# Who makes the high part: every third piece of turned probabilities read from PSUM once, and split on GpSimd

## The chip, the cores and the metric

The kernel runs on one core of one Trainium2 chip. The core has five engines, each with an instruction queue of its own that runs in order: TensorE (PE; its weight loads are shown apart as PEld), VectorE (DVE), ScalarE (ACT), GpSimd (POOL) and SyncE (SP), which issues all loads and stores here. The metric is device time in microseconds (us) of one execution; of the kernel before there are three timed runs, and one profiled execution. The programs are put in order at build time by a scheduler that fills each engine's queue; what an engine does next is fixed from then on, and semaphores make it wait where data or a buffer is missing.

## The reference

One layer of a streaming encoder with 2048 positions of width 1024, in float32. Two attention branches run beside each other and are merged:

```python
xn = rms_norm(h, norm_gain[layer])
proj = xn @ w_in[layer]                       # q, k, v, gates, indexer
ya = chunked_relpos_attention(qa, ka, va, rel_bias) * silu(ga)   # own chunk of 64 and 8 before it
yb = dsa_sparse_attention(qb, kb, vb, iq, ik, iw) * silu(gb)     # 256 keys chosen for each query
merged = sigmoid(za + b0) * (ya @ w_branch_a) + sigmoid(zb + b1) * (yb @ w_branch_b)
out = rms_norm(h + merged @ w_out[layer])
```

Both branches have 8 heads of 64. In each, for a head, scores are made, turned into probabilities by a softmax, and multiplied with the values. That last product, of probabilities and values, is where the change lies.

## The kernel before, in words

TensorE multiplies in fp32r, a float32 form that keeps fewer bits. To get float32 results, an operand is kept as two tiles, a high part (the value rounded to fp32r) and a low part (the value less its high part), and the products of the parts are added up in PSUM.

The program has three stages. Up to about 1055 us it normalizes, projects (L216) and chooses the keys of branch B. From about 1070 to 1890 us it runs attention; from there on it makes the output product (L1420). The attention stage is a list of units: `a_unit` is a group of 512 queries and one head of branch A, `b_unit` is 128 queries and two heads of branch B. Each unit has loads, a part `one` and a part `two`, and the recorded program runs `one` of the next unit beside `two` of this one.

Part `one` makes scores on TensorE (L905 for A, L1014 for B), which VectorE takes from PSUM with bias or mask into the tile P while it finds the row's extreme mx (L831); then ScalarE takes the exponential in place (L909, L1017). Only two PSUM tiles hold scores.

Part `two` needs the probabilities with keys along the partitions. TensorE turns P by transposes into a PSUM tile pt (L939, L1031; up to four blocks of 128 columns, one piece; three such tiles in rotation). The function `split` then makes the piece's high part pth and low part ptl in SBUF, and TensorE multiplies both with the values into the PSUM tile O (L949 for A, L1039 for B), high part first, piece after piece. pth and ptl have three buffers each (HB = 3).

`split` is called 432 times. In two of three calls ScalarE copies pt to pth (L854) and VectorE subtracts, reading pt again (L855). In every third call (EVERY = 3, 144 of them, called turned pieces below), GpSimd does the subtraction. GpSimd does not read PSUM in this program, so ScalarE reads pt twice: once to round it into pth (L847), once to copy it as it is into an SBUF tile pf (L848, one buffer, PFB = 1); GpSimd then subtracts (L852).

What else stands in GpSimd's queue in this stage: the low part of the branch weights (dw, L1077), sums with the other branch (dt, L1090), the row sums spread out (rb, rbb; L975, L1053), and the gate product and low part of the attention output (L980, L984, L1060, L1065). `branch` (L1071) is the product of the gated attention output with w_branch_a or w_branch_b, in chunks of 128 rows; it is given out between the units.

Of the kernel before, what the change touches and what calls it, by code (L numbers as in the profile page):

```python
# [8 lines left out]
F32 = mybir.dt.float32  # L9
# [6 lines left out]
AF = mybir.ActivationFunctionType  # L16
OP = mybir.AluOpType
# [13 lines left out]
FAR = 1e30  # L31
LGC = 1.0
YB = {"a": 1, "b": 1}
EVERY, MODE = 3, 1
PFB = 1
EARLY = 400
KVO = 6
# [10 lines left out]
SPL, LEAD = 96, 8  # L48
# [33 lines left out]
def f32(ap):  # L82
    return ap.bitcast(F32)
# [11 lines left out]
def block_kernel(ctx: ExitStack, tc: tile.TileContext, io, dbg=None):  # L95
    nc = tc.nc
# [333 lines left out]
    for p, pr in enumerate(pairs):  # L430
        for k, b in enumerate(pr):
            n = 128 * (b + 1)
# [400 lines left out]
    turn = [PH]  # L833

    def split(hi, lo, src, n):
        turn[0] += 1
        if MODE == 3:
            c = n * SPL // 128
            nc.scalar.activation(hi, src, AF.Copy)
            pf = wk.tile([128, 512], F32, name="pf", tag="pf", bufs=PFB)[:, :n - c]  # L840
            nc.scalar.activation(pf, src[:, c:], AF.Copy)
            nc.vector.tensor_tensor(lo[:, :c], src[:, :c], f32(hi[:, :c]), op=OP.subtract)
            nc.gpsimd.tensor_tensor(lo[:, c:], pf, f32(hi[:, c:]), op=OP.subtract)
        elif EVERY and turn[0] % EVERY == 0:
            pf = wk.tile([128, 512], F32, name="pf", tag="pf", bufs=PFB)[:, :n]
            if MODE == 1:
                nc.scalar.activation(hi, src, AF.Copy)  # L847
                nc.scalar.activation(pf, src, AF.Copy)  # L848
            else:
                nc.scalar.activation(pf, src, AF.Copy)  # L850
                nc.gpsimd.tensor_copy(hi, pf)
            nc.gpsimd.tensor_tensor(lo, pf, f32(hi), op=OP.subtract)  # L852
        else:
            nc.scalar.activation(hi, src, AF.Copy)  # L854
            nc.vector.tensor_tensor(lo, src, f32(hi), op=OP.subtract)  # L855
# [16 lines left out]
    def a_unit(G, h):  # L872
# [39 lines left out]
        def two():  # L912
# [20 lines left out]
            for p_ in packs:  # L933
                pt = next_pt([128, 512])
                off = 0
                for kt, j0, nj in p_:
                    for j in range(j0, j0 + nj):
                        f = max(0, 4 * G + j - 4)
                        nc.tensor.transpose(pt[:, off:off + 128], P[:, j, (kt - f) * 128:(kt - f + 1) * 128], ident)  # L939
                        off += 128  # L940
                ph_ = wk.tile([128, 512], F32R, name="pth", tag="pth", bufs=HB)
                pl_ = wk.tile([128, 512], F32R, name="ptl", tag="ptl", bufs=HB)
                split(ph_[:, :off], pl_[:, :off], pt[:, :off], off)
                yield
                off = 0
                for kt, j0, nj in p_:
                    w = nj * 128
                    for n_, src in enumerate((ph_, pl_)):
                        nc.tensor.matmul(O[:, j0 * 128:j0 * 128 + w], v[:, kt - base, :], src[:, off:off + w],  # L949
                                         start=(done == 0 and n_ == 0), stop=(done == total - 1 and n_ == 1),  # L950
                                         skip_group_check=True)
                    done += 1
                    off += w
# [32 lines left out]
    def b_unit(b, u):  # L986
# [33 lines left out]
        def two():  # L1020
# [5 lines left out]
            for kt in range(0, b + 1, 2):  # L1026
                nk = min(2, b + 1 - kt)
                pt = next_pt([128, 2, 2, 128])
                for k in range(nk):
                    for e in range(2):  # L1030
                        nc.tensor.transpose(pt[:, k, e, :], P[:, e, (kt + k) * 128:(kt + k + 1) * 128], ident)  # L1031
                ph_ = wk.tile([128, 2, 256], F32R, name="pth", tag="pth", bufs=HB)
                pl_ = wk.tile([128, 2, 256], F32R, name="ptl", tag="ptl", bufs=HB)
                split(ph_.rearrange("p k n -> p (k n)")[:, :nk * 256], pl_.rearrange("p k n -> p (k n)")[:, :nk * 256],
                      pt.rearrange("p k e n -> p (k e n)")[:, :nk * 256], nk * 256)
                yield
                for k in range(nk):
                    for n_, src in enumerate((ph_, pl_)):
                        nc.tensor.matmul(o_, vBt[:, kt + k, :], src[:, k, :], start=(kt + k == 0 and n_ == 0),  # L1039
                                         stop=(kt + k == b and n_ == 1), skip_group_check=True)  # L1040
# [484 lines left out]
```

## Time and profile before

| | |
|---|---|
| timed runs (3) | 2093.07 us median, 2090.68 to 2093.47 |
| profiled execution, own time | 2089.03 us |
| its span | 2087.2 us |
| mean granted TensorE clock | 0.987 of full speed |
| busy over the span | PE 1997.9 us (96%), PEld 1693.9 (81%), DVE 1475.8 (71%), ACT 1285.5 (62%), POOL 809.9 (39%) |

The span is the time from the first to the last instruction that the profiler shows; the execution's own time is 1.8 us longer. Durations below are of this profiled execution. Busy times count an instruction from its start to its end. TensorE's matmuls overlap in its pipeline and their ends are modelled, so its busy share can be near 100% where it could still do more. In the rows of the trace, `out<-in` are the program's tile names, x is a count, and what stands in brackets is the idle time of the engine ahead of the instruction and what ended it.

### The profile page before, as it was taken

The numbers are of one execution on the slowest core, as the hardware profiler recorded it, in microseconds if no ns is written. First come the engines' busy times: TensorE is split into PE (matmuls) and PEld (weight loads), VectorE is DVE, ScalarE is ACT, GpSimd is POOL, SyncE is SP. The second block draws the span as 40 slices with busy tenths as digits, with TensorE's granted clock in tenths as the row PEclk, the third lists the DMA queues.
The fourth block names the chain that finished last, engine by engine and source line by source line (L and its number), as shares of the span: only waits on it lengthen the run. The fifth ranks groups of instructions, "written<-read, shape, count | busy, mean of one in ns | idle before, by whom it ended". The sixth has DMA issues, their size and how long they took to land.

```text
span 2087.2 us, 33654 instructions
## 1 busy us (share of the span) xinstructions
PE 1997.9 (96%) x10706; PEld 1693.9 (81%) x10706; DVE 1475.8 (71%) x3746; ACT 1285.5 (62%) x2644; POOL 809.9 (39%) x981
## 2 busy tenths in 40 slices
PE   8798999999998999999978999999999999999998
PEld 7576888889888887888867888888888888888886
DVE  6739899989798836555546678766886688865434
ACT  5465666656565544654458779866886688873221
POOL 2146322122221345545435455445444644343410
PEclk9899999999999999999989999999999999999999
DMA  9487433354545453333485664555245631145642
GB/s 359 145 290 242 166 131 123 106 176 147 178 170 175 150 184 112 116 129 119 134 237 171 203 192 143 155 177 191 88 124 178 195 109 51 58 140 191 216 134 91
DMA packets 225928, 333.77 MB, mean 160 GB/s; under 512 B 28625, under 2 KB 99665, under 8 KB 225617
## 3 DMA queue, kind: packets, MB, share of 16 engines
q1 hardware_dynamic: 225744, 331.57, 49.2%
q8 instruction: 85, 1.39, 0.3%
q14 instruction: 99, 0.80, 0.1%
HBM read 219.33 MB, written 112.16 MB: 159 GB/s over the span
## 4 chain that ended last, share of the span: by engine, by line
PE 53%; DMA 4%; DVE 2%; ACT 2%; issue 1%; POOL 1%; SPq 1%; DVEq 0%; ACTq 0%; POOLq 0%
PE acc L216 12%; PE po L1420 9%; PE d L216 8%; PE O L1039 6%; PE s L1014 5%; PE pt L1031 5%; PE O L949 3%; PE s L905 3%; PE pt L939 3%; DMA dst<-wA 1%; DMA kk<-kA 1%; DMA dst<-wB 1%; DVE P L831 1%; DMA ost<-wO 1%; DVE ptl L855 0%
## 5 line engine op out<-in xcount | busy, mean ns | idle before, releaser
L216 PE MATMUL acc<-xh,wt 128*128 128x512 f32 x1856 | 599.3, 394 | 5.7 <-DVE e L336 2.4
L216 PEld LDWEIGHTS acc<-xh,wt 128*128 128x128 f32 x1856 | 347.2, 188 | 84.4 <-DVE e L336 2.6
L216 PE MATMUL acc<-xl,wt 128*128 128x512 f32 x928 | 363.8, 393 | 0.0
L208 POOL TENSOR_TENSOR wt<-wst,wt 128x512 fp32r<-128x512 f32 (+1 forms) x108 | 145.4, 1375 | 419.8 <-ACT wt L207 303.4
L852 POOL TENSOR_TENSOR ptl<-pf,pth 128x512 fp32r<-128x512 f32 (+1 forms) x144 | 179.6, 1247 | 178.0 <-ACT pf L848 128.4
L855 DVE TENSOR_TENSOR ptl<-pt,pth 128x512 fp32r<-128x512 f32 (+1 forms) x288 | 187.3, 660 | 45.0 <-ACT pth L854 42.5
L216 PEld LDWEIGHTS acc<-xl,wt 128*128 128x128 f32 x928 | 174.5, 188 | 38.7
L485 DVE SCALAR_TENSOR_TENSOR sc<-lg,iw,sc 128x512 f32<-128x512 f32 (+2 forms) x266 | 178.6, 678 | 26.1 <-ACT lg L480 21.9
L1014 PE MATMUL s<-kBt,qsB 128*128 128x512 f32 (+3 forms) x640 | 188.0, 385 | 1.3 <-DVE mx L831 0.9
L480 ACT ACTIVATE lg<-lg 128x512 f32<-128x512 f32 (+2 forms) x304 | 147.9, 521 | 44.5 <-PE lg L478 43.6
L854 ACT ACTIVATE pth<-pt 128x512 fp32r<-128x512 f32 (+1 forms) x288 | 159.3, 578 | 25.2 <-PE pt L939 11.5
L1017 ACT ACTIVATE P<-P,mx 128x128 f32<-128x128 f32 (+15 forms) x128 | 154.3, 1207 | 20.6 <-DVE mx L831 20.1
L1031 PE MATMUL pt<-ident,P 128*128 128x128 f32 x1088 | 164.4, 273 | 1.2 <-DVE ptl L855 0.6
L1039 PE MATMUL O<-pth,vBt 128*128 128x256 f32 x544 | 146.3, 288 | 3.2 <-ACT pth L854 1.4
L1039 PE MATMUL O<-ptl,vBt 128*128 128x256 f32 x544 | 145.8, 295 | 1.8 <-POOL ptl L852 1.2
L831 DVE CUSTOM_DVE_ANT_0 P<-s,mk,mx 128x512 f32<-128x512 f32 (+2 forms) x192 | 125.0, 651 | 29.8 <-PE s L1014 24.7
L1031 PEld LDWEIGHTS pt<-ident,P 128*128 128x128 f32 x1088 | 127.0, 140 | 10.5 <-DVE ptl L855 1.1
L1077 POOL TENSOR_TENSOR dw<-dst,dw 128x512 fp32r<-128x512 f32 x64 | 82.7, 1292 | 124.5 <-ACT dw L1076 122.7
L478 PE MATMUL lg<-ikT,iqT 128*128 128x512 f32 (+2 forms) x304 | 111.3, 378 | 18.0 <-DVE sc L485 17.9
L905 PE MATMUL s<-kk,qz 128*128 128x256 f32 (+2 forms) x464 | 113.8, 341 | 15.4 <-DMA kk<-kA 7.8
L533 ACT ACTIVATE jk<-sc,st 128x640 int8<-128x640 f32 (+6 forms) x49 | 71.2, 1453 | 84.3 <-DVE st L551 73.6
L1014 PEld LDWEIGHTS s<-kBt,qsB 128*128 128x128 f32 x640 | 102.9, 190 | 15.8 <-DVE mx L831 9.1
(286 smaller groups left out, 4738.9 us busy)
## 6 DMA issues: line engine op xcount, KB each, us to landing
wst<-wP SPq DMA_DIRECT2D x100, 256.0 KB
wst<-wS SPq DMA_DIRECT2D x56, 256.0 KB
kk<-kA SPq DMA_DIRECT2D x56, 256.0 KB
vs<-vA SPq DMA_DIRECT2D x56, 256.0 KB
qz<-qA SPq DMA_DIRECT2D x96, 128.0 KB
xrow<-x SPq DMA_DIRECT2D x16, 512.0 KB
vA<-eh SPq DMA_DIRECT2D x32, 256.0 KB
dst<-wA SPq DMA_DIRECT2D x32, 256.0 KB
```

The costliest lines, as they stand in the source:

```text
L216: nc.tensor.matmul(acc, a, b, start=(first and i == 0), stop=(last and i == n - 1), **({} if first and last else {"skip_group_check": True}))
L480: nc.scalar.activation(lg, lg, AF.Relu)
L485: nc.vector.scalar_tensor_tensor(o_, lg, wv, o_, op0=OP.mult, op1=OP.add)
L852: nc.gpsimd.tensor_tensor(lo, pf, f32(hi), op=OP.subtract)
L854: nc.scalar.activation(hi, src, AF.Copy)
L855: nc.vector.tensor_tensor(lo, src, f32(hi), op=OP.subtract)
L905: nc.tensor.matmul(s_ps[:, :w], q[:, m, j * 128:(j + 1) * 128], kk[:, ko:ko + w], start=(m == 0), stop=(m == 1))
L1014: nc.tensor.matmul(s_ps[:, :w], q[:, h, :], kBt[:, m, a:a + w], start=(m == 0), stop=(m == 1))
L1017: nc.scalar.activation(P[:, e, :n], P[:, e, :n], AF.Exp, bias=mx[:, e:e + 1], scale=-1.0, accum_out=st["sum"][:, (u % 2) * 2 + e:(u % 2) * ...
L1031: nc.tensor.transpose(pt[:, k, e, :], P[:, e, (kt + k) * 128:(kt + k + 1) * 128], ident)
L1039: nc.tensor.matmul(o_, vBt[:, kt + k, :], src[:, k, :], start=(kt + k == 0 and n_ == 0), stop=(kt + k == b and n_ == 1), skip_group_check= ...
L1420: nc.tensor.matmul(accs[t, hf], a, b[:, n_], start=(k == 0 and i == 0), stop=(k == KT - 1 and i == 2))
```

## The change

For a turned piece, ScalarE now reads pt once, as a plain copy into pf. GpSimd makes the high part from pf by a copy that rounds to fp32r (a CAST in the built program), and then the low part as before. The calls of `split` that aren't turned do what they did; branches that the settings never reach are deleted as well, so that all lines behind `split` have numbers smaller by 11 (L1039 becomes L1028, L1031 becomes L1020, L1014 becomes L1003, L852 becomes L841).

```diff
-EVERY, MODE = 3, 1
+EVERY, MODE = 3, 2
...
     def split(hi, lo, src, n):
         turn[0] += 1
...
-        elif EVERY and turn[0] % EVERY == 0:
+        if turn[0] % EVERY == 0:
             pf = wk.tile([128, 512], F32, name="pf", tag="pf", bufs=PFB)[:, :n]
-            if MODE == 1:
-                nc.scalar.activation(hi, src, AF.Copy)
-                nc.scalar.activation(pf, src, AF.Copy)
-            else:
-                nc.scalar.activation(pf, src, AF.Copy)
-                nc.gpsimd.tensor_copy(hi, pf)
+            nc.scalar.activation(pf, src, AF.Copy)
+            nc.gpsimd.tensor_copy(hi, pf)
             nc.gpsimd.tensor_tensor(lo, pf, f32(hi), op=OP.subtract)
         else:
             nc.scalar.activation(hi, src, AF.Copy)
             nc.vector.tensor_tensor(lo, src, f32(hi), op=OP.subtract)
```

Beside the 144 reads less on ScalarE and the 144 casts more on GpSimd, the scheduler puts the queues of all engines in another order from the first attention unit on; nothing moves before it.

TensorE's queue early in the stage, before the change, from the transposes of one turned piece of branch B (pt_13239, 256 columns) to the product with its high part (pth_13242):

```order
L1031 MATMUL pt_13239<-ident_103,P_13164 128x128 x2
L1039 MATMUL O_13170<-ptl_13175,vBt_12324 128x256
L1031 MATMUL pt_13325<-ident_103,P_13232 128x128 x4
L1014 MATMUL s_13347<-kBt_12323,qsB_13160 128x256 x2
L1014 MATMUL s_13361<-kBt_12323,qsB_13160 128x256 x2
L1039 MATMUL O_13170<-pth_13242,vBt_12324 128x256
```

The same place after the change:

```order
L1020 MATMUL pt_13239<-ident_103,P_13164 128x128 x2
L1028 MATMUL O_13170<-ptl_13175,vBt_12324 128x256
L1020 MATMUL pt_13325<-ident_103,P_13232 128x128 x4
L1003 MATMUL s_13394<-kBt_12323,qsB_13160 128x256 x2
L1020 MATMUL pt_13351<-ident_103,P_13318 128x128 x4
L1003 MATMUL s_13411<-kBt_12323,qsB_13160 128x256 x2
L216 MATMUL d_13035<-ya0_12543,dw_13030 128x512
L1045 MATMUL pt_13379<-ident_103,rbb_13377 128x128 x2
L1003 MATMUL s_13423<-kBt_12323,qsB_13386 128x384 x2
L1003 MATMUL s_13437<-kBt_12323,qsB_13386 128x384 x2
L1028 MATMUL O_13170<-pth_13242,vBt_12324 128x256
```

Between the transposes and the product with the high part stood four rows, and now stand nine: other scores (s), the transposes of a later piece and a matmul of `branch` (d) have moved ahead of the product.

GpSimd's queue around the same piece, before:

```order
L980 TENSOR_TENSOR y_12932<-y_12932,sg_12714 128x512
L852 TENSOR_TENSOR ptl_13243<-pf_13244,pth_13242 128x256
L1060 TENSOR_TENSOR yb_13097<-yb_13097,sgB_12869 128x256
L984 TENSOR_TENSOR ya1_12544<-y_12932,ya0_12543 128x512
L1053 COPY rbb_13377<-sumB_13234 128x256
```

And after:

```order
L1042 COPY rbb_13377<-sumB_13234 128x256
L840 CAST pth_13242<-pf_13244 128x256
L973 TENSOR_TENSOR ya1_12544<-y_12932,ya0_12543 128x512
L1049 TENSOR_TENSOR yb_13097<-yb_13097,sgB_12869 128x256
L841 TENSOR_TENSOR ptl_13243<-pf_13244,pth_13242 128x256
```

The cast stands ahead of the subtraction, not always right ahead of it: here two gate operations of finished units lie between the two.

More of the change, by code (lines that the diff above doesn't have):

```diff
@@ L836, in split @@
         turn[0] += 1
-        if MODE == 3:
-            c = n * SPL // 128
-            nc.scalar.activation(hi, src, AF.Copy)
[L840 to L843, printed above, removed]
-        elif EVERY and turn[0] % EVERY == 0:
-            pf = wk.tile([128, 512], F32, name="pf", tag="pf", bufs=PFB)[:, :n]
-            if MODE == 1:
-                nc.scalar.activation(hi, src, AF.Copy)
-                nc.scalar.activation(pf, src, AF.Copy)
-            else:
-                nc.scalar.activation(pf, src, AF.Copy)
-                nc.gpsimd.tensor_copy(hi, pf)
+        if turn[0] % EVERY == 0:
+            pf = wk.tile([128, 512], F32, name="pf", tag="pf", bufs=PFB)[:, :n]
+            nc.scalar.activation(pf, src, AF.Copy)
+            nc.gpsimd.tensor_copy(hi, pf)
             nc.gpsimd.tensor_tensor(lo, pf, f32(hi), op=OP.subtract)
```

## The prediction

> **What bounds the kernel now.** I read the page's chain first, then a table of stretches over the stage that the change touches, then what TensorE waits for in it.
>
> The chain that ended last, by engine and by line:
>
> ```profile
> PE 53%; DMA 4%; DVE 2%; ACT 2%; issue 1%; POOL 1%; SPq 1%; DVEq 0%; ACTq 0%; POOLq 0%
> PE acc L216 12%; PE po L1420 9%; PE d L216 8%; PE O L1039 6%; PE s L1014 5%; PE pt L1031 5%; PE O L949 3%; PE s L905 3%; PE pt L939 3%; DMA dst<-wA 1%; DMA kk<-kA 1%; DMA dst<-wB 1%; DVE P L831 1%; DMA ost<-wO 1%; DVE ptl L855 0%
> ```
>
> TensorE's own work is the chain. ScalarE, from which the change takes a read, holds 2% of it, and GpSimd, which receives a step, 1%. The attention stage, in which all pieces are split, in stretches (columns: length, then busy time of PE, PEld, DVE, ACT, POOL):
>
> ```profile
> core 0: us, PE busy (x) PEld busy (x) DVE busy (x) ACT busy (x) POOL busy (x), PEclk, DMA share, GB/s
> 1070.00:1150.00 80.00, 67.17 (x392) 58.77 (x392) 51.18 (x181) 62.16 (x177) 41.69 (x48) 0.88 0.62 174
> 1150.00:1250.00 100.00, 96.47 (x600) 84.33 (x599) 68.07 (x198) 74.50 (x168) 53.70 (x54) 1.00 0.67 202
> 1250.00:1350.00 100.00, 98.69 (x674) 87.36 (x673) 82.83 (x236) 91.88 (x191) 53.49 (x54) 1.00 0.47 140
> 1350.00:1450.00 100.00, 97.32 (x602) 86.28 (x601) 61.67 (x163) 64.77 (x125) 52.93 (x48) 1.00 0.63 195
> 1450.00:1550.00 100.00, 97.06 (x673) 86.17 (x672) 83.95 (x235) 88.82 (x172) 41.99 (x44) 1.00 0.34 106
> 1550.00:1650.00 100.00, 99.96 (x630) 88.35 (x629) 65.82 (x172) 69.77 (x130) 49.00 (x44) 1.00 0.56 173
> 1650.00:1750.00 100.00, 98.61 (x675) 88.10 (x674) 79.60 (x222) 83.72 (x155) 47.69 (x44) 1.00 0.36 111
> 1750.00:1800.00 50.00, 49.27 (x336) 43.78 (x335) 42.76 (x117) 43.60 (x75) 20.32 (x20) 1.00 0.12 39
> 1800.00:1890.00 90.00, 86.73 (x554) 76.35 (x553) 59.52 (x123) 65.02 (x112) 36.38 (x33) 1.00 0.40 124
> sum 820.00, PE 791.28 PEld 699.49 DVE 595.39 ACT 644.24 POOL 397.18; mean PE 87.92 PEld 77.72 DVE 66.15 ACT 71.58 POOL 44.13
> ```
>
> TensorE stands idle for 820 - 791.28 = 28.7 us, 12.8 of them in the first stretch, and 740 - 724.11 = 15.9 us in all the others together. Since a busy TensorE is not one at its peak, I check this against the weight loads: at the rate of the tightest stretch (88.35 of 100 busy) the loads after 1150 (640.72 us) would fill 725 us, 15 less than the 740 they take. Both ways, about 15 us after 1150 are to be had. ScalarE reaches 92% in one stretch, but TensorE is idle there for 1.3 us only.
>
> What TensorE waited for from 1060 to 1890 (total us, times, longest; from its weight loads, then from its matmuls from 1000 on):
>
> ```profile
> PEld s L905 <- DVE mx L831: 12.1, 18, 5.5
> PEld s L1014 <- DVE mx L831: 9.1, 26, 0.7
> PEld d L216 <- ACT dw L1076: 7.6, 7, 3.1
> PEld O L1039 <- DVE ptl L855: 5.1, 17, 0.5
> PEld O L1039 <- ACT pth L854: 3.9, 6, 1.6
> PEld O L949 <- DVE ptl L855: 3.6, 10, 0.8
> PEld O L1039 <- POOL ptl L852: 1.6, 2, 1.2
> ```
>
> ```profile
> PE s L905 <- DMA kk<-kA: 7.8, 3, 4.8
> ```
>
> Few of these waits are for a turned piece (POOL ptl, 1.6 us). Most are for VectorE, which in turn waited for ScalarE's high part, in its own row:
>
> ```profile
> DVE ptl L855 <- ACT pth L854: 42.5, 44, 4.1
> ```
>
> So ScalarE reaches TensorE in two steps at most, and thinly.
>
> **The change, part by part.** One turned piece of 512 columns, as it runs now:
>
> ```profile
> 1120.81 0.59 ACT L847 ACTIVATE pth<-pt 128x512 fp32r<-128x512 f32 x1
> 1121.29 0.60 ACT L848 ACTIVATE pf<-pt 128x512 f32<-128x512 f32 x1
> 1121.97 1.29 POOL L852 TENSOR_TENSOR ptl<-pf,pth 128x512 fp32r<-128x512 f32 x1 [0.62 <-ACT pf L848]
> ```
>
> *Removed: one PSUM read.* The second read begins 0.48 us after the first, so a piece frees 0.48 us of ScalarE, not 0.60; for 256 columns it is 0.28, from the rows of the second example below. The groups give the counts:
>
> ```profile
> L848 ACT ACTIVATE pf<-pt 128x512 f32<-128x512 f32 x132 | 78.8, 597 | 0.0
> L848 ACT ACTIVATE pf<-pt 128x256 f32<-128x256 f32 x12 | 4.6, 383 | 0.0
> ```
>
> 132 x 0.48 + 12 x 0.28 = 66.7 us. ScalarE's busy time in the stage falls from 644.2 to 577.5, its idle time rises from 175.8 to 242.5. The PSUM buffer of the piece comes free 0.48 us sooner.
>
> *Added: a cast on GpSimd.* The trace of before has no cast of that size. Its nearest rows:
>
> ```profile
> L852 POOL TENSOR_TENSOR ptl<-pf,pth 128x512 fp32r<-128x512 f32 x132 | 170.7, 1294 | 173.5 <-ACT pf L848 124.8 <-PE s L1014 19.8 <-issue 7.0
> L975 POOL COPY rb<-sum 128x512 f32<-128x512 f32 x16 | 9.8, 613 | 22.9 <-DVE sum L973 21.1 <-PE pt L939 1.6
> L1053 POOL COPY rbb<-sumB 128x256 f32<-128x256 f32 x32 | 12.8, 399 | 34.6 <-DVE sumB L1051 17.1 <-PE s L1014 8.1 <-DVE mx L831 2.7
> L852 POOL TENSOR_TENSOR ptl<-pf,pth 128x256 fp32r<-128x256 f32 x12 | 8.9, 738 | 4.5 <-ACT pf L848 3.6 <-PE s L905 0.9
> L1165 POOL CAST vBt<-mx 128x1 fp32r<-128x1 f32 x3 | 0.6, 192 | 0.0
> ```
>
> The lower end is the one-input copy, 0.61 us; the upper the two-input subtraction, 1.29. A gain is excluded on that engine, since the instruction is new there. I take 0.61: one input, and casting a single column costs 192 ns, what little instructions cost there anyway. 132 x 0.613 + 12 x 0.399 = 85.7 us (upper end 179.7): GpSimd goes from 397.2 to 483 us, 59% of the stage (70%). The Trainium skill's page "GPSIMD Engine Reference", section 4.1, speaks against such a move: it sends elementwise work on a tile to VectorE, and calls GpSimd about line rate only with one input; section 3.1 has 769 ns for a tight loop over 512 elements. By that page the cast would be an estimated 0.77 us, GpSimd would have some 23 us more to do, and the sum below would stay as it is.
>
> *Moved: when the parts are ready.* Counted from the start of ScalarE's first read, the high part is ready at 0.59 now, and then at 0.60 + 0.08 (the gap that the rows show from the copy's end to the start of GpSimd, which was idle) + 0.61 = 1.29: 0.70 later (1.38 with a cast of 1.29). The low part is ready at 1123.26 - 1120.81 = 2.45 now, and then at 1.29 + 1.29 = 2.58 to 2.66 (with one more such gap, as the subtraction now waits for its own engine's cast): 0.13 to 0.21 later (0.9 with a cast of 1.29). I cost this at nothing on the path, because the scheduler knows of the cast and has put TensorE's products behind more work, as the rows of the order show. How thin the cover is today, at the piece of those rows:
>
> ```profile
> 1130.35 0.38 ACT L847 ACTIVATE pth<-pt 128x256 fp32r<-128x256 f32 x1
> 1130.63 0.38 ACT L848 ACTIVATE pf<-pt 128x256 f32<-128x256 f32 x1
> 1130.79 0.38 PE L1039 MATMUL O<-pth,vBt 128*128 128x256 f32 x1
> ```
>
> The high part ended at 1130.73 and TensorE took it at 1130.79. In the new order five more TensorE rows stand ahead of that product, so the 0.70 us has work over it. Without cover it costs 0.70 us for each exposed piece.
>
> *Moved: the wait for a free buffer of the high part.* It goes from ScalarE's queue to GpSimd's, where behind the waiting cast stand the subtractions of the branch weights (dw) and the gate products. That frees ScalarE a little; I put no number on it beside the 67 us.
>
> *Moved: the loads.* SP's queue is reordered at the start of the stage. TensorE's waits for a load, 7.8 us for kk, are for loads that both orders issue at the same places or one row apart; I take 0, from -3 to +3.
>
> The sum: TensorE's idle time without the load's is 28.7 - 7.8 = 20.9 us. I let it shrink as ScalarE's idle time grows: 20.9 x (1 - 175.8 / 242.5) = 5.8 us gained. That proportion is a choice; its ends are nothing (windows in which ScalarE was 65 to 75% busy were no less idle on TensorE: 3.5, 2.7 and 0.0 us against 1.3, 2.9 and 1.4 in the fullest) and the whole 15.9. The profiled execution of 2089.03 us becomes 2083.2. It is 4.0 below the median of 2093.07, so against the median I say 2087.3. About 0.2%, or 4.2 us, is what a measurement of this kernel can tell from no change.
>
> **The rivals.**
>
> *Nothing comes of it.* TensorE is the chain, and the relieved engine was not what it waited for. For it: the windows just named, and the 2% of ScalarE in the chain. Against it: 42.5 us in which VectorE waited for the high part, and VectorE's row maxima are TensorE's largest waits. Time: 2093, within 4.
>
> *GpSimd's queue makes the products late.* TensorE's waits for products stand at 17 + 6 + 10 + 2 = 35 places in the rows above. If a third of them, as many as pieces are turned, meets a part that is 0.70 us later, that is 12 x 0.70 = 8.4 us: 2101.5. If the products of all 35 are dragged along, since they add to one PSUM tile in order, 35 x 0.70 = 24.5 us: 2117.6. It is fed by GpSimd's queue:
>
> ```profile
> POOL ptl L852 <- ACT pf L848: 128.4, 63, 5.3
> ```
>
> Only 63 of 144 subtractions found GpSimd idle and waiting for the copy; at the others it was mostly still at other work, and there the cast, hence the high part, now stands in line too. Against it: the longer cover in the order. It decides where TensorE reaches the high part less than 1.29 us after the copy began.
>
> That the change does not do what it says is ruled out by the order: the casts are on GpSimd, and ScalarE has one read for each turned piece.
>
> **How the numbers follow.** Forecast (gain of 4 to 16 us): 0.42. Nothing: 0.31. Late products: 0.27. The low end is the whole 15.9 us and 2 of the loads: 2075. The high end is the third rival's 2101.5 and half of the 3 for the loads: 2103. Outside I leave 0.06 below and 0.12 above. The likeliest case's own range is 2077 to 2089. Faster 0.42, same 0.31, slower 0.27.
>
> **What would show it.** Right, if in the profile after the cast takes about 0.61 us, ScalarE's busy time in the stage falls by some 67 us, VectorE's wait for the high part falls below 42.5 us, and TensorE's idle time in the stage falls to about 23 us. Wrong upward, if new waits of TensorE for the cast or for ptl of GpSimd exceed 8 us in total, or the cast takes near 1.3 us. Wrong in the way of nothing, if ScalarE's share falls as said and TensorE's idle time stays at 28 us.

## The result and the profile after

The changed kernel takes 2123.28 us (median of 4 runs, 2120.23 to 2129.63), the kernel before 2092.87 beside it: a ratio of 1.0147 [1.0126, 1.0167], 30 us slower. The profiled execution took 2124.71 us, its span is 2122.9. One of the ten runs of cast_short_plan, in the table further on, took 3262.92 us and is left out of its ratio; the other nine took 2084.06 to 2091.01.

The chain that ended last, by engine and by line, in the profile after:

```profile
PE 49%; DMA 5%; DVE 4%; ACT 2%; issue 2%; POOL 2%; SPq 1%; DVEq 0%; ACTq 0%; POOLq 0%
PE acc L216 12%; PE po L1409 7%; PE d L216 7%; PE s L1003 5%; PE O L1028 5%; PE pt L1020 4%; PE O L938 3%; PE s L894 3%; PE pt L928 2%; DVE P L831 2%; DMA ost<-wO 1%; DMA dst<-wA 1%; DMA mf<-mD 1%; DMA wst<-wS 1%; DVE ptl L844 1%
```

TensorE has 49% of the chain where it had 53, VectorE 4 where it had 2. GpSimd, which got the work, has 2 and had 1.

From its first score to its last product the attention stage takes 858.5 us (1063.3 to 1921.8), where it took 828.3 (1060.4 to 1888.7): 30.2 us more, so the whole loss lies here. (The two profiled executions are 35.7 us apart; 2.9 of these lie ahead of the stage and 2.6 behind it.) The stage in stretches, columns as before:

```profile
core 0: us, PE busy (x) PEld busy (x) DVE busy (x) ACT busy (x) POOL busy (x), PEclk, DMA share, GB/s
1070.00:1150.00 80.00, 64.20 (x354) 52.93 (x353) 46.46 (x171) 52.48 (x154) 40.08 (x50) 0.86 0.58 165
...
1250.00:1350.00 100.00, 93.91 (x602) 79.05 (x601) 74.36 (x215) 75.31 (x153) 59.72 (x67) 1.00 0.45 141
...
1830.00:1920.00 90.00, 80.59 (x504) 68.95 (x504) 54.49 (x110) 53.25 (x87) 45.25 (x46) 1.00 0.39 120
sum 850.00, PE 804.21 PEld 697.78 DVE 596.73 ACT 588.21 POOL 480.77; mean PE 89.36 PEld 77.53 DVE 66.30 ACT 65.36 POOL 53.42
```

In the first stretch TensorE gets through 354 matmuls where it did 392, and by its weight loads the stretch from 1250 and the last are looser than any behind 1150 before (79.05 of 100 and 68.95 of 90 busy). TensorE's busy time says that 850 - 804.2 = 45.8 us are idle, 17 more than before, which is only half of the loss. The weight loads tell the rest: at the rate of the tightest stretch of before (88.35 of 100 busy), 697.78 us of loads fill 790 us, so 60 of 850 are lost, where it was 820 - 792 = 28. The Trainium skill's page "Perfetto Trace Analysis", section "Identifying the Most-Contended Engine", warns of just this: matmuls are pipelined, so the busy share of the loads says more than that of the matmuls. The trace agrees: 32 us by the loads, 17 by the matmuls, against 30 measured. But the loads are as long as before in all (697.8 and 699.5 us), so their 32 us only repeat that the stage is longer. Where it is lost shows in their gaps: 99.9 us in the wait rows of the stage, where it was 66.6.

What TensorE's weight loads waited for from 1060 to 1925 (total us, times, longest):

```profile
PEld s L1003 <- DVE mx L831: 18.9, 43, 1.0
PEld s L894 <- DVE mx L831: 18.6, 35, 5.8
...
PEld po L1409 <- ACT wosy L1123: 6.5, 4, 2.2
...
PEld pt L1020 <- DVE ptl L844: 4.9, 10, 1.2
PEld pt L928 <- issue: 4.3, 7, 1.8
PEld pt L1020 <- issue: 3.2, 7, 1.4
PEld O L1028 <- DVE ptl L844: 2.6, 9, 0.4
PEld pt L928 <- DVE ptl L844: 2.4, 5, 0.9
```

Not one row of any weight stands for GpSimd (0.3 us in all for the products, 0.9 for all loads). Two kinds of wait have grown, by about as much. The scores wait for VectorE to empty one of the two PSUM tiles: 37.5 us, where it was 21.2. And the transposes wait, 27.4 us in all their rows, where it was 9.5: 7.5 us of it (1.1 before) for VectorE's subtraction, which reads the tile pt, and 9.3 us ("issue") for nothing that the profile shows. The products themselves wait less, 8.1 us and not 18.9. Before the change, rows of the transposes and of VectorE's waits for scores:

```profile
PEld pt L939 <- issue: 2.1, 1, 2.1
...
PEld pt L1031 <- DVE ptl L855: 1.1, 4, 0.5
```

```profile
DVE P L831 <- PE s L905: 50.4, 69, 4.7
...
DVE P L831 <- PE s L1014: 35.1, 62, 2.4
```

VectorE itself has not become busier (596.7 us, it had 595.4), and it waits less for the high part; after the change:

```profile
DVE P L831 <- PE s L894: 58.3, 66, 6.5
DVE P L831 <- PE s L1003: 49.6, 68, 2.8
...
DVE ptl L844 <- ACT pth L843: 12.4, 19, 2.1
```

So TensorE waits longer for VectorE to take scores, and VectorE waits longer for TensorE to make them (107.9 us, where it was 85.5). Both grow, with the same scores to make and to take: it points to scores that come less evenly, in lumps. GpSimd's cast is quick, and at 39 of the 144 pieces its engine stands idle until a product of TensorE gives back a tile pth:

```profile
L841 POOL TENSOR_TENSOR ptl<-pf,pth 128x512 fp32r<-128x512 f32 x132 | 171.2, 1297 | 7.4 <-PE O L938 1.4
L840 POOL CAST pth<-pf 128x512 fp32r<-128x512 f32 x132 | 81.9, 621 | 155.4 <-ACT pf L839 82.0 <-PE O L1028 49.3 <-PE O L938 22.4
```

One lump in the timeline (start, length, instruction, and in brackets the idle time ahead of it and what ended it):

```profile
1490.26 0.60 ACT L839 ACTIVATE pf<-pt 128x512 f32<-128x512 f32 x1 [1.60 <-PE pt L1020]
...
1491.26 0.37 PE L1028 MATMUL O<-ptl,vBt 128*128 128x256 f32 x1
...
1491.89 0.61 POOL L840 CAST pth<-pf 128x512 fp32r<-128x512 f32 x1 [2.58 <-PE O L1028]
...
1492.06 0.28 PE L1028 MATMUL O<-ptl,vBt 128*128 128x256 f32 x1
1492.18 0.62 PE L1003 MATMUL s<-kBt,qsB 128*128 128x512 f32 x2
...
1492.84 0.75 DVE L831 CUSTOM_DVE_ANT_0 P<-s,mk,mx 128x512 f32<-128x512 f32 x1 [1.03 <-PE s L1003]
...
1492.99 0.48 PE L1003 MATMUL s<-kBt,qsB 128*128 128x256 f32 x2
...
1493.65 0.30 PEld L1003 LDWEIGHTS s<-kBt,qsB 128*128 128x128 f32 x2 [0.38 <-DVE mx L831]
```

Seven products in a row come from 1491.26 on. GpSimd has stood idle for 2.58 us ahead of the cast; the copy that it needs ended at 1490.86, so the last 1.03 us were for one of these products to free a tile pth. VectorE stands 1.03 us without scores, until 1492.84; then three pairs of score matmuls come within 1.5 us, and the third waits for VectorE. In the whole of TensorE's queue the products came 3.2 in a row on the mean before, with 13 runs of 11 or more; after, 4.0 and 41 (1536 products each, counted in the built order).

### The profile page after: what moved, and what is told of

It reads as the page before. It is cut to its first block, busy times and chain, and to the rows that moved or that the text cites. A ratio compares the mean times of both kernels' runs of the same rounds, so it can differ in the third digit from the quotient of the medians.

```text
span 2122.9 us, 33698 instructions
## 1 busy us (share of the span) xinstructions
PE 2016.9 (95%) x10706; PEld 1697.5 (80%) x10706; DVE 1472.1 (69%) x3746; ACT 1231.0 (58%) x2500; POOL 892.8 (42%) x1125
## 4 chain that ended last, share of the span: by engine, by line
PE 49%; DMA 5%; DVE 4%; ACT 2%; issue 2%; POOL 2%; SPq 1%; DVEq 0%; ACTq 0%; POOLq 0%
PE acc L216 12%; PE po L1409 7%; PE d L216 7%; PE s L1003 5%; PE O L1028 5%; PE pt L1020 4%; PE O L938 3%; PE s L894 3%; PE pt L928 2%; DVE P L831 2%; DMA ost<-wO 1%; DMA dst<-wA 1%; DMA mf<-mD 1%; DMA wst<-wS 1%; DVE ptl L844 1%
## 5 line engine op out<-in xcount | busy, mean ns | idle before, releaser
L1003 PE MATMUL s<-kBt,qsB 128*128 128x512 f32 (+3 forms) x640 | 188.7, 387 | 6.4 <-DVE mx L831 6.2
L844 DVE TENSOR_TENSOR ptl<-pt,pth 128x512 fp32r<-128x512 f32 (+1 forms) x288 | 182.9, 657 | 13.4 <-ACT pth L843 12.4
L841 POOL TENSOR_TENSOR ptl<-pf,pth 128x512 fp32r<-128x512 f32 (+1 forms) x144 | 180.1, 1250 | 8.0 <-PE O L938 1.4
L1020 PE MATMUL pt<-ident,P 128*128 128x128 f32 x1088 | 161.9, 274 | 6.7 <-DVE ptl L844 4.1
L840 POOL CAST pth<-pf 128x512 fp32r<-128x512 f32 (+1 forms) x144 | 87.2, 605 | 160.9 <-ACT pf L839 85.4
L1020 PEld LDWEIGHTS pt<-ident,P 128*128 128x128 f32 x1088 | 126.1, 141 | 21.3 <-DVE ptl L844 4.9
L1028 PE MATMUL O<-pth,vBt 128*128 128x256 f32 x544 | 141.8, 285 | 0.9 <-DVE yb L1038 0.6
L1028 PE MATMUL O<-ptl,vBt 128*128 128x256 f32 x544 | 142.1, 293 | 0.4 <-DVE ptl L844 0.2
L898 ACT ACTIVATE P<-P,mx 128x640 f32<-128x640 f32 (+4 forms) x128 | 97.2, 760 | 50.4 <-DVE mx L831 49.0
```

Of the source, the lines that this page charges most:

```text
L1003: nc.tensor.matmul(s_ps[:, :w], q[:, h, :], kBt[:, m, a:a + w], start=(m == 0), stop=(m == 1))
```

## The experiments

Two tools serve nearly all of them. One is a change of the step in `split`. The other holds queues to an order taken from another program: the instructions of the two programs correspond one to one, and a dependency that orders two instructions of one queue without any semaphore is put between neighbours, at the end of the recorded block.

```diff
     dph.close()
+    traced = {i.name: i for i in nc.cur_bb.bb.instructions}
+    for names in rows_of(ORDER):
+        row = [traced[n] for n in names if n in traced]
+        for a, b in zip(row, row[1:]):
+            tc.add_manual_dep(b, a.name, NoSync)
```

Theories at the start. A: the new order costs the time, the cast itself is cheap. B: a high part that is 0.7 us later makes TensorE wait in any order. C: GpSimd's added work makes all its results late. The names D to H are given to sharper forms further on, in the expectations.

All runs in one table. The columns: who makes the turned piece's high part; whose order the queues have (own: what the build gave); products in a row, mean; us that loads of scores waited for VectorE's mx and that loads of products waited for GpSimd's pth or ptl (sums of the wait rows of each trace, 1060 to 1935); time; ratio to the kernel before of the same call. The orders "before's" and "once_scalar's" hold all queues but GpSimd's, "the change's" holds TensorE's, VectorE's and SyncE's, the stand-ins' (further on) all five; what isn't held is the build's. The kernel before took 2088.2 to 2092.9 us in these calls, so times of different calls are compared by their ratios where a few us matter.

| run | high part | order | in a row | mx | GpSimd | us | ratio |
|---|---|---|---|---|---|---|---|
| the kernel before | ScalarE | own | 3.2 | 21.2 | 1.6 | 2092.9 | |
| the change | GpSimd cast | own | 4.0 | 37.5 | 0.3 | 2123.3 | 1.0147 [1.0126, 1.0167] |
| cast_order_before | GpSimd cast | before's | 3.2 | 19.9 | 65.1 | 2143.4 | 1.0252 [1.0224, 1.0281] |
| cast_pe_order_before | GpSimd cast | TensorE before's | 3.2 | 36.1 | 53.9 | 2162.8 | 1.035 [1.0317, 1.0383] |
| once_scalar | ScalarE, from the copy | own | 3.2 | 19.4 | 2.1 | 2095.1 | 1.0015 [1.0001, 1.003] |
| spare_cast | ScalarE; idle cast on GpSimd | own | 4.2 | 34.8 | 0.0 | 2148.4 | 1.0285 [1.0254, 1.0315] |
| once_order_after | ScalarE, from the copy | the change's | 4.0 | 36.7 | 1.2 | 2135.2 | 1.0222 [1.0199, 1.0246] |
| once_order_before | ScalarE, from the copy | before's | 3.2 | 18.9 | 1.6 | 2096.1 | 1.0025 [1.0013, 1.0037] |
| cast_order_once | GpSimd cast | once_scalar's | 3.2 | 21.2 | 30.0 | 2123.1 | 1.0154 [1.0135, 1.0172] |
| spare_order_before | ScalarE; idle cast on GpSimd | before's | 3.2 | 21.9 | 15.3 | 2103.6 | 1.0063 [1.0044, 1.0083] |
| cast_first_order_before | GpSimd cast | before's, GpSimd rewritten | 3.2 | 20.2 | 25.1 | 2116.8 | 1.012 [1.0096, 1.0145] |
| before_phase | ScalarE, turn shifted | own | 3.1 | 19.2 | 1.2 | 2083.1 | 0.9959 [0.9946, 0.9972] |
| cast_phase | GpSimd cast, turn shifted | own | 3.9 | 42.7 | 2.1 | 2136.2 | 1.0213 [1.0188, 1.0237] |
| cast_two_copies | GpSimd cast, two pf | own | 3.7 | 26.0 | 0.8 | 2111.4 | 1.0097 [1.007, 1.0124] |
| cast_short_plan | GpSimd cast | short stand-in's | 3.2 | 21.4 | 1.0 | 2087.9 | 0.9981 [0.9969, 0.9993] |
| cast_short_plan_phase | GpSimd cast, turn shifted | short stand-in's | 3.2 | 21.4 | 1.6 | 2092.9 | 1.0006 [0.9993, 1.0019] |
| cast_short_plan_two | GpSimd cast, two pf | short stand-in's | 3.2 | 19.9 | 3.4 | 2091.8 | 1.0005 [0.999, 1.002] |
| cast_middle_plan | GpSimd cast | longer stand-in's | 3.5 | 30.5 | 2.6 | 2104.1 | 1.0088 [1.0059, 1.0116] |
| product_for_cast | GpSimd product | own | 3.4 | 24.2 | 3.3 | 2092.8 | 1.0019 [1.0008, 1.003] |

**The change's instructions in the order before.** cast_order_before holds the queues of TensorE, VectorE, ScalarE and SyncE; cast_pe_order_before only TensorE's.

```diff
-EVERY, MODE = 3, 1
+EVERY, MODE = 3, 2
+ORDER = the queues of the kernel before
```

> The change's instructions (one read by ScalarE, cast and subtraction on GpSimd), but the queues of TensorE, VectorE, ScalarE and SyncE are held to the order of the kernel before; only GpSimd's queue is left to the scheduler, which has to place the casts. Theory A (the new order of the queues costs the 30 us, the cast itself is cheap): 2083 to 2095 us, near the kernel before or below it. Theory B (the high part comes 0.7 us later and TensorE waits for it, whatever the order): 2115 to 2135 us, with TensorE waiting at the products O. Theory C (GpSimd's 87 us more work makes all its other results late): 2110 to 2125 us.

> The change's instructions with TensorE's queue alone held to the order of the kernel before; the other queues are the scheduler's. Theory A: if TensorE's order is what matters, 2083 to 2100 us; if it is the order on VectorE and ScalarE, near 2120 us. Theory B: 2115 to 2135 us. Theory C: 2110 to 2125 us.

Both are slower than the change, and above what any of the three theories had. A falls in this form: it had the loss vanish once the old order is back. What cast_order_before waits for (TensorE's loads):

```profile
PEld O L1039 <- POOL ptl L852: 30.2, 24, 4.0
PEld O L1039 <- POOL pth L851: 19.5, 25, 2.8
PEld s L905 <- DVE mx L831: 12.5, 21, 4.7
PEld O L949 <- POOL pth L851: 11.7, 8, 4.1
PEld s L1014 <- DVE mx L831: 7.4, 20, 0.7
```

The waits for mx are back at 19.9, and 65 us for GpSimd have come in their place. The order of the change does cover GpSimd's lateness, as the prediction said; what the cover costs, the next runs ask.

**Lateness alone, load alone.** In once_scalar, ScalarE rounds the high part from its own copy, so it is later, with nothing more on GpSimd. In spare_cast the high part is made as before, and GpSimd makes a cast that nobody reads ahead of each of its subtractions.

```diff
 once_scalar
-                nc.scalar.activation(hi, src, AF.Copy)
                 nc.scalar.activation(pf, src, AF.Copy)
+                nc.scalar.activation(hi, pf, AF.Copy)
 spare_cast
                 nc.scalar.activation(pf, src, AF.Copy)
+            nc.gpsimd.tensor_copy(wk.tile([128, 512], F32R, name="sp", tag="sp", bufs=1)[:, :n], pf)
             nc.gpsimd.tensor_tensor(lo, pf, f32(hi), op=OP.subtract)
```

> No cast on GpSimd: ScalarE copies the turned piece from PSUM to pf once and then rounds pf, in SBUF, into the high part; GpSimd subtracts as before. The PSUM tile comes free as early as in the change, the high part comes about 0.5 us later than before, ScalarE's work stays. The scheduler orders anew. Theory A: between the two kernels, 2095 to 2115 us, as the scheduler sees a smaller delay and moves less. Theory B: about 0.5/0.7 of the loss, 2110 to 2116 us. Theory C: 2088 to 2097 us, as GpSimd has no more work than before.

> The kernel before with the cast added on GpSimd in front of each subtraction, written to a spare tile that nothing reads; the high part still comes from ScalarE's first read. GpSimd has the change's load, the high part is not late, the low part is about 0.6 us later. Theory A: depends on how the scheduler reorders for the later low part; 2090 to 2110 us. Theory B: 2090 to 2100 us, since only the low part is later. Theory C: 2110 to 2125 us.

Over the 144 turned pieces, the high part is ready 2.33 us after the copy began in once_scalar (mean; 0.58 before, 2.07 with the change) and the low part 3.91 (2.69, 4.09). It is as late as with the change, at a cost of 0.15%: B, which had 2110 to 2116, falls for an order that is made for it. spare_cast, whose high part isn't late at all, is some 25 us slower than the change and above what any theory had, with the change's marks and without a wait for GpSimd:

```profile
PEld s L1015 <- DVE mx L831: 19.2, 40, 1.3
PEld s L906 <- DVE mx L831: 15.6, 26, 5.4
```

That left C, or an order that goes wrong as soon as a cast stands on GpSimd (D). The next four cross instructions with orders; each edit is one of those above with an ORDER from another row of the table.

> The second copy on ScalarE (the high part rounded by ScalarE from the copy, no cast on GpSimd), but with the queues of TensorE, VectorE and SyncE held to the order of the change. Theory D (the order into which the build puts the queues once a cast stands on GpSimd costs the time): 2110 to 2125, most of the change's 30 us, though GpSimd has no cast to do. Theory C (GpSimd's 87 us of added work costs the time): under 2100, as with the same instructions in their own order (2095).

> The same instructions as in the run before this one, with the queues of TensorE, VectorE, ScalarE and SyncE held to the order of the kernel before. The high part is some 0.5 us later than before and nothing in the order makes room for it. Theory E (a late high part costs wherever the order has no cover): 2097 to 2110, with new waits of TensorE's products for ScalarE's high part. Theories C and D: 2090 to 2095.

> The change's instructions (cast on GpSimd), with the queues of TensorE, VectorE, ScalarE and SyncE held to the order that the build gives when ScalarE rounds the copy, which has room for a high part that is half a microsecond late, and took 2095 there. Theory D: 2093 to 2103. Theory C: 2120 or more. Theory E lies between, by the 0.1 to 0.5 us that the cast is later than ScalarE's rounding: 2100 to 2115, with TensorE waiting for GpSimd's cast.

> The kernel before with a GpSimd cast into a tile that nobody reads ahead of each of its subtractions (2148 in the order that the build gave it), now with the queues of TensorE, VectorE, ScalarE and SyncE held to the order of the kernel before. The high part comes from ScalarE as before, the low part is 0.6 us later. Theory D: 2090 to 2105. Theory C: 2120 or more, with TensorE waiting for GpSimd's low part.

once_order_after has no cast at all and takes 2135 in the change's order (D had 2110 to 2125), with the change's waits:

```profile
PEld s L1014 <- DVE mx L831: 19.5, 41, 1.0
PEld s L905 <- DVE mx L831: 17.2, 33, 5.0
```

spare_order_before has the whole added load of GpSimd, and costs 0.6% in the order before where it cost 2.9 in its own. So the order costs the time without the cast, and most of what C claimed falls. The 2135 is not the price of the order alone, though: ScalarE, whose queue is not held, has the rounding to do there, for which the order was not made. once_order_before gives the price of a later high part without cover: it is ready at 1.23 us (mean), 0.65 later, at all 144 pieces, and costs 0.25% or 5 us, between E's 2097 and the others' 2095; TensorE's loads wait 9.1 us, at 20 places, for it. cast_order_once went against D and E: 2123, as only C had it, with 30 us of waits for GpSimd in an order that is good for ScalarE's rounding.

**Where the casts stand in GpSimd's queue; other orders; a second copy.** In cast_order_before the cast began within 0.15 us of the copy's end at 87 pieces only; at 50 it stood behind other GpSimd work, most of it the branch weights' subtraction (L1077) and the sums (L1090), some of which itself waited. cast_first_order_before writes out GpSimd's queue too, with those 50 casts moved to where their copy ends and each subtraction right behind its cast. Two runs shift the turn by one piece (`PH` from 2 to 0), which gives a wholly new order with the same instructions, and one gives pf two buffers (`PFB = 2`).

> The change's instructions with the queues of TensorE, VectorE, ScalarE and SyncE held to the order of the kernel before (2143 with GpSimd's queue left to the build). Now GpSimd's queue is written out too: the 50 casts that the trace of that run showed standing behind other GpSimd work while their copy was ready are moved ahead of it, and every subtraction follows its cast at once. Theory F (the casts' places in GpSimd's queue made the products late): 2095 to 2112, and TensorE's waits for GpSimd in the stage fall from 62 us to under 25. Rival (a high part that is 0.7 us late at the least has no room in that order, wherever the cast stands): 2130 or more.

> The kernel before with the turn shifted by one piece, so that the first GpSimd piece is the third and not the first; the same instructions, but the build gives the queues another order throughout. Theory D1 (orders are much alike in worth unless a cast stands on GpSimd): 2085 to 2100. Theory D2 (an order that is made anew can be tens of us worse whatever the instructions): 2105 or more is possible.

> The change with the same shift of the turn. Theory D1: 2110 to 2130, some 20 to 35 above the shifted kernel before. Theory D2: it can fall anywhere from 2090 to 2140, and its distance to the shifted kernel before is no longer 30.

> The change with two buffers for ScalarE's copy instead of one, in the order that the build gives it. If ScalarE's queue, held up by the one buffer until GpSimd's subtraction is done, makes up a good part of the loss: 2112 or less. Theory D1 or D2: 2110 to 2135, no clear gain over the change's 2123.

GpSimd's queue accounts for half of the loss in the old order: 2143 becomes 2117, between the two expectations, and TensorE waits 25 us for GpSimd and not 65. The rows left are those of the high part, with its median of 1.28 us:

```profile
PEld O L1039 <- POOL pth L851: 14.7, 24, 1.6
...
PEld O L949 <- POOL pth L851: 8.6, 8, 3.5
```

D1 holds in its direction only: the shifted kernel before is not spoilt by its new order (2083, the fastest of all here, and below D1's 2085), while the shifted change is 53 us above it, more than the 20 to 35 expected, and above D1's 2130. For the shifted change D2 was nearer, which had up to 2140 and a distance other than 30. Two copies take 10 to 12 us off the change, at the edge where both expectations meet, though the high part is then twice as late (4.4 us, mean); the runs of products are shorter (3.7). Whether the single pf or the new order did that was not separated.

**A shorter step in the plan.** The build orders the queues before anything runs, so by its own idea of how long an instruction takes. The question was whether it takes the cast to be longer than it is (H). A stand-in program is built that has another GpSimd instruction in the cast's place; its order is taken for all five queues, and the change's instructions run in it. The stand-in itself never runs.

```diff
 stand-in for cast_short_plan, cast_short_plan_phase, cast_short_plan_two
-                nc.gpsimd.tensor_copy(hi, pf)
+                nc.gpsimd.tensor_tensor(hi[:, :n // 2], pf[:, :n // 2], pf[:, :n // 2], op=OP.mult)
 stand-in for cast_middle_plan
-                nc.gpsimd.tensor_copy(hi, pf)
+                nc.gpsimd.tensor_tensor(hi, pf, pf, op=OP.mult)
 product_for_cast (runs itself, unit is a column of ones)
-                nc.gpsimd.tensor_copy(hi, pf)
+                nc.gpsimd.tensor_tensor(hi, pf, unit.to_broadcast([128, n]), op=OP.mult)
```

> The change's instructions, with all five queues held to an order that the build gave a stand-in program in which each cast is a GpSimd instruction that the build's plan holds for shorter (a product of two operands over half the columns, which the chip ran in 0.74 us against the cast's 0.61). Theory H (the build plans the cast as far longer than it runs, and so draws TensorE's products together into long runs): in this order the runs of products are as short as before (3.2 on the mean, against 4.0 with the change and 3.2 before), and the time is 2088 to 2104. Theory G (a high part that comes from GpSimd, 1.3 us after the copy began or later when GpSimd is at other work, costs in any order): 2110 or more, with TensorE waiting for GpSimd.

> The same for the turn shifted by one piece, where the kernel before took 2083 and the change 2136. Theory H: 2080 to 2097. Theory G: 2110 or more.

> The same as the first of these with two buffers for ScalarE's copy. Theory H: 2084 to 2102, and no more than the first. Theory G: 2105 or more.

> The change's instructions again, held to the order that the build gives a second stand-in: a GpSimd product of two operands over the whole piece, an instruction of the kind that takes 1.30 us here. Runs of products in this order are 3.5 on the mean, between those of the shorter stand-in (3.2) and of the change (4.0). Theory H (the longer the build takes the step to be, the longer the runs, and these cost the time): between 2088 and 2123, about 2100. If the orders differ in worth by accident alone, it can be as low as 2088 or above 2123.

> The change with the cast spelled as a GpSimd product of the copy with one, in the order that the build itself gives. GpSimd's step takes about 1.3 us instead of 0.61, so GpSimd has some 99 us more to do than with the change, and the high part is 0.7 us later still. The build's order has runs of products of 3.4. Theory H: 2100 to 2118, below the change's 2123 although the step is twice as long. Theory C (GpSimd's work): 2135 or more.

With the very instructions of the change, the short plan takes 2088, 2093 and 2092, where the build's own orders take 2123, 2136 and 2111. H had all three to within a microsecond, but not that the third, with two buffers pf, be no slower than the first: where the order fits, one buffer is enough. The waits of cast_short_plan are those of the kernel before, and its last product ends 38 us earlier than the change's (1883.8, 1921.8):

```profile
PEld s L905 <- DVE mx L831: 13.1, 17, 5.5
PEld s L1014 <- DVE mx L831: 8.3, 21, 1.0
```

```profile
1150.00:1885.00 735.00, 720.64 (x4713) 638.87 (x4711) 541.49 (x1454) 523.31 (x984) 432.20 (x469) 1.00 0.46 144
sum 815.00, PE 789.41 PEld 698.77 DVE 596.43 ACT 584.26 POOL 479.56; mean PE 394.71 PEld 349.38 DVE 298.21 ACT 292.13 POOL 239.78
```

The high part is ready at 1.89 us here (mean), later than in cast_order_before (1.60), and TensorE waits 1 us for GpSimd in place of 65: it isn't how late a part comes that costs, but how late against where its product stands. The middle dose falls between on both counts (3.5 in a row, 2104). And product_for_cast puts a longer step on GpSimd than the change:

```profile
L853 POOL TENSOR_TENSOR pth<-pf,unit 128x512 fp32r<-128x512 f32 x132 | 137.4, 1041 | 147.0 <-ACT pf L852 84.3 <-PE O L1041 38.4 <-PE s L1016 9.4
```

It takes 1041 ns (1300 was expected) against the cast's 621; GpSimd is busy for 58 us more of the stage (539.2 to 480.8), and the kernel is some 27 us faster than the change by the ratios, in the order that the build itself gave. C had 2135 or more. That finishes C, as the short plan did G. H had the right side but not the size: it expected 2100 to 2118.

What is shown: the same instructions gain 35 us by the order alone (2123.3 and 2087.9), and the order follows the instruction that stands in the plan. Which of the five queues does it was not separated. That the build takes the cast for longer than a two-operand instruction is inferred from its longer runs (4.0, against 3.5 and 3.4); how long it takes it to be, no run here shows.

## Why the prediction was wrong

*The PSUM read.* Forecast 66.7 us less of ScalarE in the stage; it fell from 644.2 to 588.2, by 56. The order of size was right. In the trace the durations of ScalarE's instructions in the stage add up to 746.0 us before and 656.1 after, 90 less, but they also overlap 34 us less (101.8 and 67.9); the forecast took off the overlap of the two reads with each other only.

*The cast.* Right: 0.621 us and 87 us in all, against 0.61 and 85.7; GpSimd reached 480.8 us, forecast 483. By the Trainium skill's page "GPSIMD Engine Reference", section 3.1, the estimate was 0.77, so the measurement stands below the 769 ns that the page calls its best case. (The 23 us more that the prediction worked out from it count all 144 pieces as 512 wide; for 132 it is 21.)

*VectorE's wait for the high part.* Right: it fell from 42.5 to 12.4 us. It bought nothing: TensorE's waits for VectorE grew all the same.

*When the parts are ready.* Forecast 0.70 us later for the high part and 0.13 to 0.21 for the low one. On the mean it is 1.5 and 1.4 (0.58 to 2.07, 2.69 to 4.09). The forecast counted a cast that finds GpSimd idle; at more than half of the pieces it stood behind other work or waited for a tile pth. GpSimd's idle time that ended with such a tile is 73.8 us, of which 19.2 came after the copy was ready; the prediction had named this wait and left it without a number:

```profile
POOL pth L840 <- PE O L1028: 51.3, 28, 4.9
...
POOL pth L840 <- PE O L938: 22.5, 11, 3.4
```

*The cover.* Here the prediction failed: "I cost this at nothing on the path, because the scheduler knows of the cast and has put TensorE's products behind more work". The products did stand behind more work, and they did not wait for GpSimd, 0.3 us in all. But the rows that stood ahead of the product were taken as free. TensorE adds the products of a unit in order, so one that is put back dams up those behind it; they come out in long runs (4.0 on the mean, and 3.2 before), hold the three tiles pth and ptl for longer (ScalarE's waits for a tile pth that a product still held rose from 11.0 to 23.9 us), and leave the scores to come in lumps, which VectorE takes one at a time from two PSUM tiles. With pth not free, the split that reads pt is late too, and the transposes wait. That the order costs the time is shown: the same instructions take 2087.9 in the short plan's order and 2123.3 in this one. The way from long runs to the waits is read from the rows, and not tested: no run changed the runs of products alone, and in cast_pe_order_before the scores waited 36.1 us for VectorE with runs of 3.2. The cover was also longer than the step needed, as the short plan shows. ScalarE's largest waits of this kind, before and after:

```profile
ACT pth L847 <- PE O L1039: 8.8, 16, 1.8
```

```profile
ACT pth L843 <- PE O L1028: 14.8, 21, 1.7
...
ACT pth L843 <- PE O L938: 9.1, 8, 2.3
```

*The gain.* 20.9 x (1 - 175.8 / 242.5) let TensorE's idle time shrink with ScalarE's. ScalarE's idle time grew to 261.8 us and TensorE's grew too, to 45.8. The proportion had no mechanism behind it. With a fitting order the same change is worth 0.2% one way (cast_short_plan against before) or, with the turn shifted, 10 us the other way (2092.9 against 2083.1): the rival "nothing comes of it" describes the instructions well.

*The loads.* Right: TensorE's wait for kk is 6.8 us, and was 7.8.

*The late products.* This rival ended on the right side by another road: its sign, waits for GpSimd over 8 us, is not in the profile after. Its price was of the right size: 8.4 us for 12 exposed pieces that are 0.70 late, against 5 us measured for 0.65, with waits at 20 places (once_order_before). With the cast on GpSimd in the old order the price is 53 us, since GpSimd's queue adds a tail to the lateness: half of it goes when the casts stand first.

Nothing in the profile of before could show this. The new order could: the products in a row were there to be counted, 3.2 and 4.0. Over the runs in which the products wait at most 3.4 us for GpSimd, the time follows that count, which was first made after the result was known: 3.1 to 3.2 in a row took 2083 to 2096, 3.4 to 3.5 took 2093 to 2104, 3.7 took 2111, 3.9 to 4.2 took 2123 to 2148.

## What to carry to other kernels

Where a scheduler rewrites the queues, predict the new order, not only the new step: count how long the runs of each kind of instruction have become on the engine that bounds the kernel, and ask what sits idle during a run. A cover that the scheduler adds is paid for, here at least, by what it pushes together. To tell step and order apart, run the new instructions in an old order and the old instructions in the new one; and if the order is at fault, another spelling of the step can mend it even when that spelling is slower by itself (2092.8 with a 1.04 us step, 2123.3 with one of 0.62).

## What the runs showed of the hardware

GpSimd's product of a full operand with one column, spread over the row, took 1041 ns for 512 columns where the subtraction of two full operands took 1304 in the same program.

VectorE's subtraction and its reduction did not slow down with GpSimd's added 84 us beside them. Before the change and after:

```profile
L855 DVE TENSOR_TENSOR ptl<-pt,pth 128x512 fp32r<-128x512 f32 x260 | 176.2, 686 | 44.2 <-ACT pth L854 41.9 <-POOL dt L1090 0.8 <-PE s L905 0.5
L831 DVE CUSTOM_DVE_ANT_0 P<-s,mk,mx 128x512 f32<-128x512 f32 x104 | 77.6, 746 | 20.0 <-PE s L1014 17.6
```

```profile
L844 DVE TENSOR_TENSOR ptl<-pt,pth 128x512 fp32r<-128x512 f32 x260 | 172.8, 684 | 12.9 <-ACT pth L843 12.0
L831 DVE CUSTOM_DVE_ANT_0 P<-s,mk,mx 128x512 f32<-128x512 f32 x104 | 77.6, 747 | 25.6 <-PE s L1003 21.9
```

The Trainium skill's page "SBUF — State Buffer", section "Who interferes with whom", has the two engines contend for a read port only where VectorE takes two operands from SBUF (or runs in a two-port mode). Both of these take one from PSUM, and 686 and 684, 746 and 747 ns agree; the other case was not tried.
